# Nine of 256 softmax score units taken from ScalarE and computed on VectorE

## The chip, the cores and the metric

The kernel runs on one core of a Trainium2 chip. Its time is the device time of one execution in microseconds; most executions of one kernel agree within a few tenths of a per cent, but some, whatever the kernel, are some 3% longer. Medians below are over all executions of a kernel. A **ratio** is the mean time of one kernel's fast runs over the mean of the other kernel's fast runs of the same rounds, with a 95% interval, so it is not quite the ratio of the medians quoted beside it. "Span" is the time from the first to the last instruction of the one profiled execution; it is some 2 us below the time.

## The reference

Softmax attention over 64 heads of 512 x 64, in fp32:

```python
scale = 1.0 / np.sqrt(q.shape[-1])
scores = np.einsum('bhqd,bhkd->bhqk', q, k) * scale
scores = scores - scores.max(axis=-1, keepdims=True)
attn = np.exp(scores)
attn = attn / attn.sum(axis=-1, keepdims=True)
return np.einsum('bhqk,bhkd->bhqd', attn, v)        # 8 x 8 x 512 x 64
```

## The kernel before

Two heads make a pair; there are 32 pairs. A **unit** is one block of 128 keys against the 512 queries of one head: a 128x512 block of transposed scores, eight units to a pair, 256 in all. Three units make a group. TensorE writes the group's scores (`st`, two such buffers in PSUM, the memory that its results land in), ScalarE turns them into fp16 exponentials (`pt`) with one activation of 128x1536 into SBUF, the other on-chip memory, and TensorE later multiplies them with the values (`o`). VectorE copies transposed queries and keys out of PSUM (`tqk<-tps`) and normalises the outputs (`rcp`, `osb`); GpSimd casts the inputs to fp16.

```python
G = 3
def aux(shape, dt, name):                 # transposes AND outputs: two buffers, taken in turn
    return pspool.tile(shape, dt, tag="ps_x", bufs=2, name=name)
def scores(j):
    st[j] = pspool.tile([P, G, S], FP32, tag="ps_st", bufs=2, name=f"st_{j}")
    ...                                   # one matmul per unit into st[j][:, x, :]
def softmax(j):
    pt[j] = ppool.tile([P, G, S], FP16, tag="pt", name=f"pt_{j}")
    nc.scalar.activation(out=pt[j][:, 0:n], in_=st[j][:, 0:n], func=EXP, scale=scale)
def attend(g, h):
    o = aux([P, NI, W], FP32, f"o_{g}_{h}")
    weigh(g, h, o, range(NI))             # 16 matmuls pt x v; column 64 of v is 1: the sum
    normalise(g, h, o)                    # VectorE: reciprocal, then a multiply
...
for j, n in enumerate(sizes[:-1]):        # the program order of every engine
    softmax(j)
    scores(j + 1)
    ...                                   # work gets transposes and outputs as they fall due
    credit = min(credit + 0.42 * n, 2.0)
    while work and (credit >= 1.0 or j > len(sizes) - 6):
        f, *a = work.popleft(); f(*a); credit -= 1.0
```

The softmax here doesn't subtract the row's maximum and nothing guards it: scores larger than these inputs give would overflow.

## Time and profile before

| | before |
|---|---|
| time, median (lowest to highest) | 127.5 us (126.45 to 129.82), 3 runs |
| span of the profiled run | 125.1 us |
| ScalarE busy; idle before its exponentials | 117.5 us, 94%; 1.0 us |
| TensorE, VectorE, GpSimd busy | 107.2, 60.7, 58.9 us |

The prediction below shows the lines on which its reading rests. Two rows more, the busy tenths in 40 slices of the span, tell the room that the change wants to use. In this part of the page each digit is the busy share of one fortieth of the span, 9 meaning 90% or more:

```profile
DVE  0344536553653745445454554645546563553450
ACT  4499999999999999999999999999999999999970
```

ScalarE has no slice under 90% between the opening and the end, and VectorE stands at about half everywhere.

In an undisturbed stretch of this kernel activations start 1.33 us apart. From the starts in a trace I work out the **lateness**: the time between one full activation's start and the next, less 1.333 us, summed over all full groups but the first. It is 0.62 us for the kernel before. Three groups fewer save 4.03 us (the prediction's figure), so a changed kernel breaks even at a lateness of 0.62 + 4.03 = 4.65 us.

### The profile page before, as it was taken

The page shows a single profiled execution, that of the slowest core. Times are in us where ns is not written, and L with a number is a line of the kernel's source. Part 1 is how long each engine was busy: PE and PEld are TensorE (multiplying, and loading weights), DVE is VectorE, ACT ScalarE, POOL GpSimd, SP SyncE. Part 2 cuts the span into 40 slices and gives each one's busy share as a digit, 9 for nine tenths or more (in the row PEclk, how much of TensorE's full clock was granted, in tenths as well). Part 3 has the DMA queues.
Part 4 walks back from the last instruction along what each step waited for, and adds up shares of the span by engine and source line. Part 5 has one row for each costly group of instructions (what it writes and reads, how often), then busy time and mean ns, then how long its engine had stood idle before and what let it go on. Part 6 is the DMA issues. An engine that isn't in the chain of part 4 may idle for free.

```text
span 125.1 us, 3986 instructions
## 1 busy us (share of the span) xinstructions
PE 107.2 (86%) x1572; PEld 63.9 (51%) x1572; DVE 60.7 (49%) x173; ACT 117.5 (94%) x93; POOL 58.9 (47%) x101
## 2 busy tenths in 40 slices
PE   6999979889997987999798798979979898997780
PEld 6636536455464454565455265545536455554450
DVE  0344536553653745445454554645546563553450
ACT  4499999999999999999999999999999999999970
POOL 2188878576565173376347523644753753000000
PEclk9999999999999999999999999999999999999999
DMA  3999999999997699999789878989999974222222
GB/s 111 290 354 350 349 350 370 365 372 375 359 355 220 177 298 332 368 341 330 219 252 364 284 246 212 368 278 289 375 302 282 350 262 147 89 84 86 89 78 89
DMA packets 34882, 33.81 MB, mean 270 GB/s; under 512 B 2096, under 2 KB 34864, under 8 KB 34864
## 3 DMA queue, kind: packets, MB, share of 16 engines
q1 hardware_dynamic: 34576, 33.30, 82.0%
q8 instruction: 12, 0.20, 0.7%
q10 hardware_dynamic: 288, 0.26, 0.6%
q14 instruction: 6, 0.05, 0.1%
HBM read 25.17 MB, written 8.39 MB: 268 GB/s over the span
## 4 chain that ended last, share of the span: by engine, by line
ACT 74%; issue 16%; PE 4%; DMA 2%; DVE 1%
ACT pt L166 74%; DMA raw<-in_k_dram 2%; PE open L139 1%; PE st L161 1%; PE o_last L174 1%; PE o L174 0%; PE st L239 0%; DVE osb L188 0%; DVE x L135 0%; DVE rcp L187 0%
## 5 line engine op out<-in xcount | busy, mean ns | idle before, releaser
L166 ACT ACTIVATE pt<-st 128x1536 f16<-128x1536 f32 (+2 forms) x88 | 115.1, 1597 | 1.0 <-PE st L161 1.0
L161 PE MATMUL st<-tqk 64*128 64x512 f16 x248 | 49.6, 380 | 13.1 <-ACT pt L166 11.5
L174 PEld LDWEIGHTS <-pt 128*128 128x128 f16 x1024 | 33.8, 98 | 18.0 <-issue 16.2
L174 PE MATMUL o<-vp,pt 128*128 128x65 f16 x1008 | 38.4, 194 | 0.0
L91 POOL CAST qk<-q 128x512 f16<-128x512 f32 x31 | 19.1, 616 | 27.4 <-DMA q<-in_q_dram 19.6
L187 DVE RECIPROCAL rcp<-o 128x4 f32<-128x4 f32 x63 | 11.3, 180 | 38.8 <-PE o L174 38.8
L120 DVE COPY tqk<-tps 128x1024 f16<-128x1024 f16 (+1 forms) x32 | 21.5, 675 | 15.4 <-PE tps L119 15.4
L188 DVE TENSOR_TENSOR osb<-o,rcp 128x256 f32<-128x256 f32 x63 | 26.7, 425 | 2.2
L100 POOL CAST vp<-v 128x512 f16<-128x512 f32 x32 | 19.8, 619 | 10.6 <-DMA v<-in_v_dram 6.4
L161 PEld LDWEIGHTS <-tqk 64*128 64x128 f16 x248 | 11.6, 93 | 23.4 <-issue 14.8
L91 POOL CAST qk<-k 128x512 f16<-128x512 f32 x31 | 19.1, 616 | 5.6 <-DMA k<-in_k_dram 4.7
L119 PEld LDWEIGHTS <-qk 128*128 128x128 f16 x248 | 13.9, 98 | 13.1 <-issue 9.3
L119 PE MATMUL tps<-ident,qk 128*128 128x128 f16 x248 | 19.2, 220 | 0.0
L239 PE MATMUL warm<-blank 128*128 128x128 f16 x24 | 2.7, 310 | 1.0 <-DVE small L226 1.0
L239 PEld LDWEIGHTS <-blank 128*128 128x128 f16 x28 | 2.8, 142 | 1.2 <-DVE small L226 1.0
L227 ACT ACT_TABLE_LOAD x1 | 1.3, 1283 | 1.7 <-PEq L314 1.7
L161 PE MATMUL st<-t,r 64*128 64x512 f16 x6 | 2.0, 381 | 0.0
L139 PE MATMUL open<-ident,x 128*64 128x128 f16 x16 | 1.7, 268 | 0.2 <-DVE x L135 0.2
L135 DVE CAST x<-raw 128x192 f16<-128x192 f32 (+1 forms) x2 | 0.6, 284 | 2.5 <-DMA raw<-in_k_dram 2.5
L135 POOL CAST x<-raw 128x192 f16<-128x192 f32 x1 | 0.3, 344 | 3.0 <-DMA raw<-in_k_dram 3.0
L139 PEld LDWEIGHTS <-x 128*64 128x64 f16 x16 | 1.3, 138 | 0.9 <-DVE x L135 0.4
L144 DVE COPY t<-open 64x384 f16<-64x384 f16 (+1 forms) x2 | 0.8, 416 | 1.7 <-PE open L139 1.7
(20 smaller groups left out, 6.5 us busy)
## 6 DMA issues: line engine op xcount, KB each, us to landing
v<-in_v_dram SPq DMA_DIRECT2D x32, 256.0 KB, 5.6
q<-in_q_dram SPq DMA_DIRECT2D x31, 256.0 KB, 5.2
k<-in_k_dram SPq DMA_DIRECT2D x31, 256.0 KB, 5.6
out_dram<-osb SPq DMA_DIRECT2D x31, 256.0 KB, 4.8
raw<-in_k_dram ACTq DMA_DIRECT2D x2, 128.0 KB, 2.9
raw<-in_q_dram SPq DMA_DIRECT2D x2, 128.0 KB, 2.8
out_dram<-osb SPq DMA_DIRECT2D x2, 128.0 KB, 1.7
```

Source lines behind the costliest of these rows:

```text
L91: nc.gpsimd.tensor_copy(out=qk[:, n].rearrange("p i (h d) -> p i h d", d=D), in_=raw[g, "qk"[n]].rearrange("p h (i d) -> p i h d", d=D),)
L100: nc.gpsimd.tensor_copy(out=vps[g % NV][:, :, :, 0:D], in_=raw[g, "v"].rearrange("p h (i d) -> p h i d", d=D),)
L119: nc.tensor.transpose(ps[:, n - lo, i, :], halves[g][:, n, i, :], ident16)
L120: nc.vector.tensor_copy(out=turned[g][:, lo:hi], in_=ps)
L139: nc.tensor.transpose(ps[:, i - lo, :], raw["x", h][:, i, :], ident16)
L161: nc.tensor.matmul(st[j][:, x, :], key, tq, start=True, stop=True)
L166: nc.scalar.activation(out=pt[j][:, 0:n], in_=st[j][:, 0:n], func=EXP, scale=scale)
L174: nc.tensor.matmul(o[:, i, :], pt[j][:, x, i * P : (i + 1) * P], vps[g % NV][:, h, c, :], start=(c == 0 and i == blocks[0]), stop=(c == NI ...
L187: nc.vector.reciprocal(out=rcp[:, lo:hi], in_=o[:, lo:hi, D:W])
L188: nc.vector.tensor_tensor(out=o_sb[g][:, h, lo:hi], in0=o[:, lo:hi, 0:D], in1=rcp[:, lo:hi].broadcast_to([P, hi - lo, D]), op=AluOp.mult,)
L227: nc.scalar.activation(out=small, in_=small, func=EXP, scale=scale)
L239: nc.tensor.matmul(tile[:, G - 1, 0:P], blank, blank, start=True, stop=True)
```

## The change

Unit 0 of the first head of pairs 4, 7, ..., 28 leaves its group. Its scores go to one `aux` buffer and its exponential is made by five VectorE operations and one GpSimd operation: n is the exponent in half octaves (int8), e the bits of that power of two, f the fraction, and a, f2 and pa a cubic in f times the power. The work is begun two pairs ahead of the output that takes it, one step per group. It also puts a due transpose at the head of the queue of work and lets that queue run faster (0.5 for 0.42).

```diff
+    aside = [(g, 0, 0) for g in range(4, last, 3)]
+    units = [u for u in units if u not in aside]
...
+    def exp_aside(g):
...
+        s = aux([P, S], FP32, f"sa_{g}")
+        nc.tensor.matmul(s, tk[:, c * P : (c + 1) * P], tq, start=True, stop=True)
+        rate = 2.0 * scale * LOG2E
+        nc.vector.tensor_scalar(out=n, in0=s, scalar1=rate, scalar2=SHIFT, ...)        # n
+        nc.gpsimd.tensor_scalar(out=e, in0=n, scalar1=float(1 << 22), ...)             # e
+        step(f, s, rate, n, AluOp.mult, AluOp.subtract)                                # f
+        yield
+        step(a, f, EXP_P, f)                                                           # a
+        yield
+        step(f, f, EXP_R, e.bitcast(FP32))                                             # f2
+        yield
+        step(out16, a, EXP_Q, f)                                                       # pa
...
-                        work.append((transpose, g + 2))
+                        work.appendleft((transpose, g + 2))
+                    if r == 4 and any(a[0] == g + 2 for a in aside):
+                        work.append((begin_aside, g + 2))
...
-            credit = min(credit + 0.42 * n, 2.0)
+            while steps and next(steps[0], 1) == 1:      # one step, ahead of this group's work
+                steps.popleft()
+            credit = min(credit + 0.5 * n, 2.0)
```

More of the change, by code (lines that the diff above doesn't have):

```diff
@@ L11 @@
 FP16 = mybir.dt.float16
+I32 = mybir.dt.int32
+I8 = mybir.dt.int8
 EXP = mybir.ActivationFunctionType.Exp
 AluOp = mybir.AluOpType
+EXP_P, EXP_Q, EXP_R = 2.28771887, 28.39494972, 3.73321451
+SHIFT = -0.8899647686
+LEAD_BITS = 1008370304
+LOG2E = 1.4426950408889634
 @with_exitstack
@@ L47 @@
             units += [(g, c, h) for c in range(NI) for h in range(2)]
+    aside = [(g, 0, 0) for g in range(4, last, 3)]
+    units = [u for u in units if u not in aside]
     n_units = len(units)
+    first_of = {g: next(n for n, u in enumerate(units) if u[0] == g) for g in range(n_pairs)}
     G = 3
@@ L161, in scores, with tmp, step, begin_aside @@
             nc.tensor.matmul(st[j][:, x, :], key, tq, start=True, stop=True)
+    apart = {}
+    def exp_aside(g):
+        _, c, h = unit = next(u for u in aside if u[0] == g)
+        tq, tk = tqk[g, h]
+        def tmp(nm, dt=FP32):
+            return ppool.tile([P, S], dt, tag=nm, bufs=3, name=f"{nm}_{g}")
+        n, e, f, a = tmp("n", I8), tmp("e", I32), tmp("f"), tmp("a")
+        out16 = tmp("pa", FP16)
+        s = aux([P, S], FP32, f"sa_{g}")
+        nc.tensor.matmul(s, tk[:, c * P : (c + 1) * P], tq, start=True, stop=True)
+        rate = 2.0 * scale * LOG2E
+        nc.vector.tensor_scalar(
+            out=n, in0=s, scalar1=rate, scalar2=SHIFT, op0=AluOp.mult, op1=AluOp.add
+        )
+        nc.gpsimd.tensor_scalar(
+            out=e,
+            in0=n,
+            scalar1=float(1 << 22),
+            scalar2=float(LEAD_BITS),
+            op0=AluOp.mult,
+            op1=AluOp.add,
+        )
+        def step(o, x, k, y, op0=AluOp.add, op1=AluOp.mult):
+            nc.vector.scalar_tensor_tensor(out=o, in0=x, scalar=k, in1=y, op0=op0, op1=op1)
+        step(f, s, rate, n, AluOp.mult, AluOp.subtract)
[5 more added lines that the diff above has]
+        step(out16, a, EXP_Q, f)
+        apart[unit] = out16
+        yield
+    steps = deque()
+    def begin_aside(g):
+        steps.append(exp_aside(g))
+        next(steps[-1])
     def softmax(j):
@@ L171, in weigh @@
         for c in chunks:
-            j, x = where[g, c, h]
+            p = apart.get((g, c, h))
+            if p is None:
+                j, x = where[g, c, h]
+                p = pt[j][:, x]
             for i in blocks:
@@ L175, in weigh @@
                     o[:, i, :],
-                    pt[j][:, x, i * P : (i + 1) * P],
+                    p[:, i * P : (i + 1) * P],
                     vps[g % NV][:, h, c, :],
@@ L280 @@
                     g, c, h = units[u]
-                    r = u % UPP
+                    r = u - first_of[g]
                     if r == 0:
```

## The prediction

> **What bounds the kernel now.** I read the page's busy shares first, then the chain that ended last, the groups of instructions, and last the timeline of one steady stretch.
>
> ```profile
> PE 107.2 (86%) x1572; PEld 63.9 (51%) x1572; DVE 60.7 (49%) x173; ACT 117.5 (94%) x93; POOL 58.9 (47%) x101
> ...
> ACT 74%; issue 16%; PE 4%; DMA 2%; DVE 1%
> ...
> L166 ACT ACTIVATE pt<-st 128x1536 f16<-128x1536 f32 (+2 forms) x88 | 115.1, 1597 | 1.0 <-PE st L161 1.0
> L161 PE MATMUL st<-tqk 64*128 64x512 f16 x248 | 49.6, 380 | 13.1 <-ACT pt L166 11.5
> L187 DVE RECIPROCAL rcp<-o 128x4 f32<-128x4 f32 x63 | 11.3, 180 | 38.8 <-PE o L174 38.8
> L120 DVE COPY tqk<-tps 128x1024 f16<-128x1024 f16 (+1 forms) x32 | 21.5, 675 | 15.4 <-PE tps L119 15.4
> L188 DVE TENSOR_TENSOR osb<-o,rcp 128x256 f32<-128x256 f32 x63 | 26.7, 425 | 2.2
> ```
>
> ScalarE's exponentials are the bound: 94% busy, idle 1.0 us before 88 instructions, and they are the chain. Its 16% "issue" is the overlap of one activation with the next, not idling: the chain shows 1.0 us of an activation, then 0.3 of issue. Full groups of three units start at 65.67 us and, 39 groups later, at 118.07, so a group takes 52.4/39 = 1.344 us. VectorE is half idle, mostly for outputs of the matmuls. That is the room the change wants.
>
> But TensorE has less room than 86% suggests. This is its timeline, then VectorE's (start, length, instruction):
>
> ```profile
> 57.17 1.16 PE L174 MATMUL o<-vp,pt 128*128 128x65 f16 x32
> 58.27 0.60 PE L161 MATMUL st<-tqk 64*128 64x512 f16 x3
> 58.80 0.62 PE L119 MATMUL tps<-ident,qk 128*128 128x128 f16 x8
> 59.35 0.60 PE L161 MATMUL st<-tqk 64*128 64x512 f16 x3
> 60.68 0.59 PE L161 MATMUL st<-tqk 64*128 64x512 f16 x3 [0.73 <-ACT pt L166]
> ```
> ```profile
> 57.88 0.18 DVE L187 RECIPROCAL rcp<-o 128x4 f32<-128x4 f32 x1 [0.70 <-PE o L174]
> 58.09 0.42 DVE L188 TENSOR_TENSOR osb<-o,rcp 128x256 f32<-128x256 f32 x1
> 58.44 0.17 DVE L187 RECIPROCAL rcp<-o 128x4 f32<-128x4 f32 x1
> 58.64 0.42 DVE L188 TENSOR_TENSOR osb<-o,rcp 128x256 f32<-128x256 f32 x1
> 59.46 0.69 DVE L120 COPY tqk<-tps 128x1024 f16<-128x1024 f16 x1 [0.39 <-PE tps L119]
> ```
>
> The chain has activations starting at 54.93, 56.26, 57.59 and 58.96. Scores (st) have two buffers, so a group's scores start 0.385 us after the start of the activation that follows the buffer's reader (60.68 against 60.30), need 0.60 plus 0.09 to hand over, and must be ready 1.33 after that start. With 32 output matmuls between (57.17 to 58.27) the scores end at 58.87 and the activation starts at 58.96, 1.37 rather than 1.33 after the one before. So in those groups TensorE is already exactly on time: a delay there is lost to ScalarE one for one. Elsewhere slack is 0.2 to 0.7 us.
>
> **What the Trainium skill says.** "ScalarE: Activation LUTs", section "What ACT_TABLE_LOAD costs": 186 ns plus 0.833 ns an element, about 93 of it overlapping, so 1373 ns for 1536 elements; the trace has 1344, near enough, and nearly all per element, so fewer units pay in proportion. "VectorE: DVE Perf Modes", section "The TRN2 errata": fp32 tensor_tensor takes (N+151)/0.96 ns. For N=256 that is 424; the trace has 425. For N=512 I take 691 as an estimate from the same formula for all five added VectorE operations. "SBUF — State Buffer", section "Who interferes with whom": a VectorE operation with two SBUF inputs and a GpSimd operation that reads SBUF exclude one another for a whole instruction. The kernel before has no such large VectorE operation (its inputs come from PSUM), so its trace can't show this.
>
> **The change, part by part.** Removed: nine units leave ScalarE, 247 remain, 80 full groups for 83. Saved: 3 x 1.344 = 4.03 us, 3.2% of the span. Alone this gives 127.5 - 4.0 = 123.5.
>
> Added per aside: one score matmul (about 0.2 us), five VectorE operations of 0.69, 3.45 us, and one GpSimd operation which I take at a cast's 0.62. VectorE grows by 31 to about 92 us, 75%; but three pairs hold one aside, whose own load (6 normalisations of 0.6 and 3 copies of 0.69, 5.7 us) plus 3.45 is 9.1 of 23/3 x 1.33 = 10.2 us, 90%. GpSimd grows by 5.6 us and has time; it runs some pairs ahead of TensorE, so a wait for n costs it nothing that matters. Transfers run five pairs ahead and stay hidden.
>
> Moved: the aside's scores take one of only two PSUM buffers that transposes and outputs use in turn. So a transpose or output now waits for VectorE to finish with the aside two allocations earlier, and its in-order queue delays the copies and normalisations that free the others. The instruction order of the built kernel shows three patterns, each three times. I walk each with trace durations: a VectorE operation starts 0.04 after the matmul's end, 0.03 after one it depends on, 0.08 before the end of an independent one; TensorE follows VectorE by about 0.1. "Late" is against 1.33 a group.
>
> Pattern one (pairs 10, 19, 28): transpose, then the aside's scores at once, then a group's scores. Let the earlier group's scores start at 0; the next (1.33) is followed by the transpose at 1.85, copied 2.51 to 3.20. The aside's scores need that copy, so they start at 3.33 and hold the following group to 3.55, ready 4.24, due 3.605: **late 0.63**. Then n 3.75 to 4.44, f to 5.16, a to 5.88, normalisation of the first output to 6.43. The second output waits for that output's buffer: 6.53 to 7.08, then scores, ready 7.77, due 6.90: **late 0.87**.
>
> Pattern two (pairs 4, 13, 22): a group lies between transpose and aside, so the copy is nearly done. Aside at 1.98, n and f to 3.81, the second output waits until 3.91, group ready at 5.13, due 4.94: **late 0.20**. The next transpose waits for the normalisation behind a, but its group is ready at 6.42, due 6.46.
>
> Pattern three (pairs 7, 16, 25): it follows 32 output matmuls, so the transpose is late and the aside waits until 3.62. Groups ready 5.08 for 4.97, 6.77 for 6.41, and, since f2 stands before the next copy, 9.72 for 9.43: **late 0.11, 0.36 and 0.29**.
>
> Sum of one of each: 1.50 + 0.20 + 0.76 = 2.46 us. Nine pairs then take 23 x 1.33 + 2.46 + 0.1 (outputs as before) = 33.15 us, against 24 x 1.344 = 32.26. Times three: 2.7 us more, which gives 130.2. Port conflicts with the casts that GpSimd has queued behind e can only add; I give them 0.3.
>
> **The rivals.** First, all hidden: 123.5 us. For it: VectorE idles half of the time, each chain has over 5 us before its output, and a transpose now goes ahead of other work. Against it: that lead protects the finished exponential alone, not the PSUM buffers and the in-order queue in between, and ScalarE has only two score buffers. Second, a break-even near 127: my first lateness in pattern one is sure by the order, but the others depend on VectorE starting each operation at once and on 0.69 us; were these some 15% shorter, most of patterns two and three would vanish, leaving 3 x 1.4 against 4.0 saved. Someone chose nine units and these places, which speaks for a version that was at least no loss. Third, port conflicts in full: GpSimd has waited for n with two pairs' casts of 0.62 behind it, just where a, f2 and the last step run. A wait of up to 0.62 before a or f2 passes into the buffers; at 0.3 for each aside it adds 2.7 us, 133. Fourth, a bound by VectorE: 90% locally is below one, so it would show as waits, not as a full engine.
>
> **Range and chances.** I take 130.5 us. The range 126.0 to 134.0 reaches from most lateness absent to conflicts in full. Two per cent either way is 124.95 and 130.05. Faster needs under a quarter of the summed lateness (1.5 of 7.4 us), and pattern one's first wait alone takes 1.9: 0.08. Within 2% needs up to 2.55 us net loss, just under my sum: 0.42. Slower: 0.50.
>
> **What would show each step.** ScalarE should have 80 full activations and a busy time about 4 us lower, and its idle time before them, by score matmuls, should rise from 1.0 to some 7 us, in stretches of 0.2 to 0.9 near each aside, longest at pairs 10, 19 and 28. TensorE should wait for VectorE at the aside's scores, after a transpose's copy, and at outputs. VectorE's added operations should read near 0.69 us; if a, f2 and the last step read longer, or casts longer than 0.62, the port rule is at work. VectorE should be near 92 us. The prediction is wrong if ScalarE's idle stays under 3 us (buffers came free sooner than I walked), if the added operations are much shorter or longer, or if TensorE waits for GpSimd's casts or for transfers, which I left out.

## The result and the profile after

The changed kernel took 131.35 us (130.85 to 132.16, 4 runs), the kernel before on the same chip 127.17 (126.45 to 129.82, 4 runs). The ratio is 1.036 [1.029, 1.042]: slower by 3.6%.

From the page of the changed kernel: the busy shares, the two rows of tenths, the chain that ended last by engine, and five groups of instructions (busy us, mean ns, then idle before and what ended it).

```profile
PE 108.8 (84%) x1572; PEld 64.0 (49%) x1572; DVE 94.3 (73%) x218; ACT 115.7 (89%) x90; POOL 73.4 (57%) x110
...
DVE  0345579869967986996897599689779958974451
ACT  4499999999899699999997988999999899699970
...
DVE 41%; PE 32%; ACT 12%; issue 10%; DMA 2%; ACTq 0%
...
L226 ACT ACTIVATE pt<-st 128x1536 f16<-128x1536 f32 (+2 forms) x85 | 113.3, 1422 | 7.4 <-PE st L175 6.4
...
L205 DVE SCALAR_TENSOR_TENSOR f<-f,e 128x512 f32<-128x512 f32 x9 | 9.9, 1105 | 0.0
L205 DVE SCALAR_TENSOR_TENSOR pa<-a,f 128x512 f16<-128x512 f32 x9 | 9.5, 1057 | 0.0
L192 DVE TENSOR_SCALAR n<-sa 128x512 int8<-128x512 f32 x9 | 6.2, 692 | 4.3 <-PE sa L190 4.3
...
L205 DVE SCALAR_TENSOR_TENSOR a<-f 128x512 f32<-128x512 f32 x9 | 6.3, 706 | 0.2
```

The chain is no longer ScalarE's (74% before, 12% now) but runs through VectorE and TensorE. ScalarE waits 7.4 us for scores where it waited 1.0. VectorE's row now has nines, several in a row with eights: 73% is an average of full and half-empty slices. And f2 and pa take 1.1 us each where n, of the same 512 columns, takes 0.69.

Next, TensorE's waits in the changed kernel (what waited, for what: us in total, times, longest).

```profile
PE sa L190 <- DVE tqk L134: 3.9, 9, 0.8
PE tps L133 <- DVE rcp L250: 3.1, 9, 0.4
PE o L237 <- DVE f L205: 2.2, 6, 0.4
PE o L237 <- DVE tqk L134: 2.1, 6, 0.5
PE o L237 <- DVE osb L251: 2.0, 3, 0.7
```

In the kernel before, the same view had 0.3 us of waits for VectorE outside the opening (the scores for `tqk`) and 11.5 us of waits for ScalarE, which are the harmless ones. Here all but the first line are waits for an `aux` buffer.

Three timelines of the aside of pair 10, first TensorE, then VectorE, then GpSimd (start, length, instruction, idle before it):

```profile
40.03 0.39 PE L190 MATMUL sa<-tqk 64*128 64x512 f16 x1 [0.79 <-DVE tqk L134]
...
41.93 0.61 PE L133 MATMUL tps<-ident,qk 128*128 128x128 f16 x8 [0.15 <-DVE f L205]
43.21 0.67 PE L237 MATMUL o<-vp,pt 128*128 128x65 f16 x16 [0.68 <-DVE osb L251]
43.81 0.82 PE L175 MATMUL st<-tqk 64*128 64x512 f16 x6
```
```profile
40.45 0.69 DVE L192 TENSOR_SCALAR n<-sa 128x512 int8<-128x512 f32 x1 [0.48 <-PE sa L190]
41.18 0.69 DVE L205 SCALAR_TENSOR_TENSOR f<-sa,n 128x512 f32<-128x512 f32 x1
41.91 0.69 DVE L205 SCALAR_TENSOR_TENSOR a<-f 128x512 f32<-128x512 f32 x1
42.52 0.18 DVE L250 RECIPROCAL rcp<-o 128x4 f32<-128x4 f32 x1
42.73 0.42 DVE L251 TENSOR_TENSOR osb<-o,rcp 128x256 f32<-128x256 f32 x1
43.07 1.10 DVE L205 SCALAR_TENSOR_TENSOR f<-f,e 128x512 f32<-128x512 f32 x1
```
```profile
41.23 0.62 POOL L195 TENSOR_SCALAR e<-n 128x512 int32<-128x512 int8 x1 [4.49 <-PE o L237]
41.92 1.15 POOL L105 CAST qk<-q 128x512 f16<-128x512 f32 x1
43.02 0.61 POOL L105 CAST qk<-k 128x512 f16<-128x512 f32 x1
```

Read them together. The first output's matmuls are long done (they start at 40.57), but its normalisation stands behind n, f and a and ends at 43.15. Only then may the second output take that buffer, at 43.21; the scores that come after it on TensorE start at 43.81, and ScalarE's next activation starts at 44.51 after 0.98 us of idling. From n at 40.45 VectorE then works until 47.40 (46.98 + 0.42, its last normalisation) without a wait that the view lists; it is the same at pairs 19 and 28. GpSimd has stopped for n (4.49 us idle) and starts a row of casts at 41.92, some of which collide with a, f2 and pa: this q cast reads 1.15 us, f2 1.10.

By the activations' starts, the lateness rose from 0.62 to 9.19 us. More lateness 8.57, less 4.03 saved, is 4.5 us; the spans differ by 129.6 - 125.1 = 4.5. The account closes; what remains is which part of the aside makes the lateness. One candidate falls away by the trace: transposes did not wait for GpSimd's casts, although these come later than before. After the opening each cast of keys was done 3.3 us or more before the transposes that read it.

### The profile page after: what moved, and what is told of

Same layout as the page of the kernel before. It is cut to its first block, busy times and chain, and to the rows that moved or that the text cites. A ratio compares the mean times of both kernels' runs of the same rounds, so it can differ in the third digit from the quotient of the medians.

```text
span 129.6 us, 4031 instructions
## 1 busy us (share of the span) xinstructions
PE 108.8 (84%) x1572; PEld 64.0 (49%) x1572; DVE 94.3 (73%) x218; ACT 115.7 (89%) x90; POOL 73.4 (57%) x110
## 4 chain that ended last, share of the span: by engine, by line
DVE 41%; PE 32%; ACT 12%; issue 10%; DMA 2%; ACTq 0%
ACT pt L226 12%; PE st L175 10%; DVE f L205 10%; PE o L237 9%; DVE osb L251 9%; PE tps L133 8%; DVE tqk L134 7%; DVE pa L205 5%; DVE n L192 5%; DVE rcp L250 3%; PE sa L190 3%; DVE a L205 2%; DMA raw<-in_k_dram 2%; PE open L153 1%; PE o_last L237 1%
## 5 line engine op out<-in xcount | busy, mean ns | idle before, releaser
L175 PE MATMUL st<-tqk 64*128 64x512 f16 x239 | 47.6, 382 | 2.1 <-ACT pt L226 1.5
L105 POOL CAST qk<-q 128x512 f16<-128x512 f32 x31 | 25.0, 805 | 2.8 <-DMA q<-in_q_dram 1.8
L114 POOL CAST vp<-v 128x512 f16<-128x512 f32 x32 | 25.1, 786 | 0.6
L195 POOL TENSOR_SCALAR e<-n 128x512 int32<-128x512 int8 x9 | 5.6, 621 | 33.5 <-PE o L237 13.5
L205 DVE SCALAR_TENSOR_TENSOR f<-f,e 128x512 f32<-128x512 f32 x9 | 9.9, 1105 | 0.0
L205 DVE SCALAR_TENSOR_TENSOR pa<-a,f 128x512 f16<-128x512 f32 x9 | 9.5, 1057 | 0.0
L192 DVE TENSOR_SCALAR n<-sa 128x512 int8<-128x512 f32 x9 | 6.2, 692 | 4.3 <-PE sa L190 4.3
L190 PE MATMUL sa<-tqk 64*128 64x512 f16 x9 | 3.5, 387 | 3.9 <-DVE tqk L134 3.9
L205 DVE SCALAR_TENSOR_TENSOR a<-f 128x512 f32<-128x512 f32 x9 | 6.3, 706 | 0.2
L205 DVE SCALAR_TENSOR_TENSOR f<-sa,n 128x512 f32<-128x512 f32 x9 | 6.2, 692 | 0.3
## 6 DMA issues: line engine op xcount, KB each, us to landing
raw<-in_k_dram ACTq DMA_DIRECT2D x2, 128.0 KB, 2.9
raw<-in_q_dram SPq DMA_DIRECT2D x2, 128.0 KB, 2.7
out_dram<-osb SPq DMA_DIRECT2D x2, 128.0 KB, 1.7
```

The lines of the kernel that those rows point to most:

```text
L105: nc.gpsimd.tensor_copy(out=qk[:, n].rearrange("p i (h d) -> p i h d", d=D), in_=raw[g, "qk"[n]].rearrange("p h (i d) -> p i h d", d=D),)
L114: nc.gpsimd.tensor_copy(out=vps[g % NV][:, :, :, 0:D], in_=raw[g, "v"].rearrange("p h (i d) -> p h i d", d=D),)
L175: nc.tensor.matmul(st[j][:, x, :], key, tq, start=True, stop=True)
L190: nc.tensor.matmul(s, tk[:, c * P : (c + 1) * P], tq, start=True, stop=True)
L192: nc.vector.tensor_scalar(out=n, in0=s, scalar1=rate, scalar2=SHIFT, op0=AluOp.mult, op1=AluOp.add)
L205: nc.vector.scalar_tensor_tensor(out=o, in0=x, scalar=k, in1=y, op0=op0, op1=op1)
```

## The experiments

Theory: the lateness comes from VectorE's in-order queue together with the two `aux` buffers, as the walk in the prediction has it. Rivals: the port collisions with GpSimd (the two engines shutting one another out of SBUF, as the prediction has it); VectorE's load by itself; the aside's own matmul and PSUM buffer; the placing of the steps. Twelve runs, with the kernel before at 126.95 (first four), 127.18 (next three), 126.71 (next three) and 126.76 us (last two). Three are not in the table, as their profiled executions were slow or had a lowered clock: tail_gpsimd, one_read and steps_last.

| run | time, us | ratio | span | VectorE time of one aside | lateness |
|---|---|---|---|---|---|
| before | - | - | 125.1 | 0 | 0.62 |
| changed | 131.35 | 1.036 | 129.6 | 4.25 | 9.19 |
| all_short | 123.07 | 0.970 | 121.5 | 1.51 | 1.10 |
| tail_short | 126.22 | 0.995 | 124.1 | 2.59 | 3.97 |
| no_exponent | 129.92 | 1.024 | 128.0 | 3.91 | 8.01 |
| apart_turn | 130.42 | 1.025 | 128.4 | 4.47 | 8.17 |
| load_only | 128.15 | 1.011 | 126.8 | 4.03, no PSUM buffer | 2.07 |
| bits | 128.56 | 1.014 | 126.5 | 2.87 | 6.35 |
| bits_apart | 126.77 | 0.999 | 125.4 | 3.03 | 5.21 |
| one_step | 123.02 | 0.971 | 121.3 | 0.69 | 1.10 |
| bits_last | 125.52 | 0.991 | 124.2 | 3.01 | 4.06 |

The fifth column is the sum of the mean durations of the added VectorE operations. In every row the span differs from that of the kernel before by the added lateness less 4.03 (load_only: without that saving), to within 0.5 us. TensorE's waits for `aux` buffers go with the lateness: 9.9 us in the changed kernel, 7.2 in no_exponent, 6.2 in bits, 2.6 in tail_short, none in one_step. (In load_only 4.3 us of them cost less, 2.07 in all.)

### All steps short (all_short)

The order of the changed kernel, all six steps on 16 columns, the outputs fed from a fixed tile. Its output is wrong, which doesn't matter for the time.

```diff
-            return ppool.tile([P, S], dt, tag=nm, bufs=3, name=f"{nm}_{g}")
+            return ppool.tile([P, 16], dt, tag=nm, bufs=3, name=f"{nm}_{g}")
...
-        apart[unit] = out16
+        apart[unit] = fixed16
```

> Wrong result on purpose: the nine asides keep their matmul, their place and their buffers, but all six steps on VectorE and GpSimd work on 16 columns of 512, and the outputs take a fixed tile. My theory (the loss is TensorE waiting for VectorE, for the aside's own buffer and behind the aside's operations) leaves only the wait of the aside's scores for the transpose's copy, some 0.2 to 0.6 us in three or six of nine places: 124 to 126.5 us, faster than before. The rival, that the extra matmul out of its group and the lost order on TensorE cost it whatever VectorE does, expects 129 or more.

Measured: 123.07 us (122.81 to 123.28), ratio 0.970 [0.967, 0.973], better than the 124 to 126.5 expected. The aside's matmul, its buffer, its place in every queue and its number of instructions cost only 1.10 - 0.62 = 0.5 us of lateness. The saving of 4.0 us is real, and the loss is in the length of the steps.

### Only n and f long (tail_short)

n and f whole, the other four on 16 columns. Its output is wrong, which doesn't matter for the time.

```diff
-        step(a, f, EXP_P, f)
+        step(a[:, 0:16], f[:, 0:16], EXP_P, f[:, 0:16])
         (e, f2 and pa likewise; the outputs take the fixed tile)
```

> Wrong result on purpose: n and f, which read PSUM, stay whole; e, a, f2 and the last step work on 16 columns. By the same walk as in the prediction: pattern one 0.63 + 0.29, pattern two 0.20, pattern three 0.11 + 0.36, 1.6 us for three asides, 4.8 for nine, against 4.0 saved: about 128 us. If only the hold of the PSUM buffer by n and f counts, it stays at 130 to 131; if only the tail counts (its length and the port conflicts), it falls to 125 or below.

Measured: 126.22 us (125.93 to 126.47), ratio 0.995 [0.992, 0.999]; lateness 3.97. That is 1.8 us below the 128 of the walk. Lengthening n and f adds 2.9 us, and giving a, f2, pa and e their length adds the other 5.2.

### No GpSimd step (no_exponent)

The exponent's step left out, so GpSimd neither waits for n nor piles up casts; f2 takes a fixed tile for e. Its output is wrong, which doesn't matter for the time.

```diff
-        nc.gpsimd.tensor_scalar(out=e, in0=n, ...)
...
-        step(f, f, EXP_R, e.bitcast(FP32))
+        step(f, f, EXP_R, fixed)
```

> Wrong result on purpose: the GpSimd step is gone and f2 multiplies with a fixed tile, so GpSimd never stops for n and has no queue of casts behind it; all five VectorE operations stay whole. If the port conflicts (f2 at 1.10 and the last step at 1.05 us for 0.69) are the main loss, these fall to 0.69 and the time to 127 or below. My theory takes them for a smaller part: 2.5 us lateness for three asides as walked, 7.4 for nine, 130 us, with f2 and the last step somewhere between 0.69 and 1.1.

Measured: 129.92 us (129.76 to 133.87), ratio 1.024 [1.021, 1.027], as expected; lateness 8.01. Two rows of its groups:

```profile
L197 DVE SCALAR_TENSOR_TENSOR pa<-a,f 128x512 f16<-128x512 f32 x9 | 8.0, 887 | 0.0
L197 DVE SCALAR_TENSOR_TENSOR f<-f,fixed 128x512 f32<-128x512 f32 x9 | 7.5, 837 | 0.0
```

The two fall from 1057 and 1105 ns, not to 692, and a rises from 706 to 805; my reading is that ordinary casts still collide with them. The stop and the casts behind it cost 9.19 - 8.01 = 1.2 us. That is a part, and not the main one; what the collisions that are left cost, no run shows.

### The tail on GpSimd (tail_gpsimd)

A right result: f2 and pa as two GpSimd operations each, to take them off VectorE.

```diff
-        step(f, f, EXP_R, e.bitcast(FP32))
+        nc.gpsimd.tensor_scalar(out=f, in0=f, scalar1=EXP_R, scalar2=None, op0=AluOp.add)
+        nc.gpsimd.tensor_tensor(out=f, in0=f, in1=e.bitcast(FP32), op=AluOp.mult)
         (pa likewise)
```

> Right result: f2 and the last step go to GpSimd as two operations each[...], VectorE keeps n, f and a, 2.1 us for each aside. Walk: pattern one 1.50, two 0.20, three 0.47, 2.2 us for three asides, 6.5 for nine against 4.0 saved: 129.5 us. If GpSimd gets too late with its casts (5.6 + 0.6 + 3.4 = 9.6 us for three pairs of 10.3) then TensorE's transposes wait for it and the time is 131 or above.

Measured: 156.41 us (151.82 to 160.5); all its runs had a lowered clock (0.89 in the profiled one), so no ratio is given. A miss by 20%, and the profile says why:

```profile
L211 POOL TENSOR_SCALAR f<-f 128x512 f32<-128x512 f32 x9 | 13.5, 1497 | 0.0
...
L212 POOL TENSOR_TENSOR f<-f,e 128x512 f32<-128x512 f32 x9 | 11.4, 1269 | 0.7
```

I had taken 0.62 us from GpSimd's casts; with fp32 in these operations take 1.27 to 1.50, while the casts in the same run still take 0.62 to 0.72. GpSimd is busy for 114 us and TensorE waits 17.8 us for pa. GpSimd has no room for this.

### The steps after the group's work (steps_last)

The next step of a begun aside stands behind the normalisations and copies of its group instead of before.

```diff
-            while steps and next(steps[0], 1) == 1:
-                steps.popleft()
+            begun = len(steps)
...                                  (after the loop over work)
+            if begun and next(steps[0], 1) == 1:
+                steps.popleft()
```

> Right result, same instructions and same load of VectorE as the changed kernel; only a, f2 and the last step stand at the end of their group's work, not at its head, so in pattern one a comes after the first output's normalisation and in pattern three f2 after the transpose's copy. My theory (an in-order VectorE in front of PSUM buffers) takes about 0.7 us off each pattern one and 0.7 to 1.0 off each pattern three, 4.2 to 5 us in all: 126 to 127.5 us. If VectorE's load as such is the loss, wherever it stands, it stays at 130 to 131.

Measured: 130.54 us, ratio 1.026 [1.022, 1.031]. Three runs lie between 130.01 and 130.73; the fourth, which is the profiled one, took 229.26 with 512-column score matmuls of 723 ns instead of 382, so its trace is not used. Less than 1% better than the changed kernel, where 126 to 127.5 us was expected: a miss.

### No aside in a transpose's group (apart_turn)

As steps_last, and an aside is put off by a group where a transpose has just been made, so its scores do not wait for that copy.

```diff
+                if work[0][0] is begin_aside and turned_now:
+                    break
```

> Right result; as the run with the steps last, and an aside no longer begins in the group that has a transpose, so its scores do not stand on TensorE right behind the copy that they need (pattern one becomes like pattern three). Theory: 0.2 to 0.6 us less for each of the three places: 0.6 to 1.8 us below the run with the steps last. If that wait is hidden anyway, no difference.

Measured: 130.42 us (129.69 to 132.97), ratio 1.025 [1.019, 1.031]; lateness 8.17, now in many pieces, most of 0.2 to 0.6 us. It is 0.1 us from steps_last, where 0.6 to 1.8 was expected. a, f2 and pa read 1.00, 1.07 and 1.02 us: later steps meet more casts (my reading). VectorE works from 28.48 to 36.5 us with one gap of 0.19, and in front of outputs TensorE's weight loads wait 4.6 us for pa, its matmuls 1.7. Moving the steps moved the lateness; neither of the two places tried had 4.5 us of VectorE to spare.

### One read of PSUM (one_read)

As apart_turn, but VectorE only copies the scaled scores to SBUF and GpSimd makes n from the copy, so the `aux` buffer is free after 0.7 us.

```diff
-        nc.vector.tensor_scalar(out=n, in0=s, ...)
+        nc.vector.tensor_scalar(out=xs, in0=s, scalar1=rate, scalar2=None, op0=AluOp.mult)
+        nc.gpsimd.tensor_scalar(out=n, in0=xs, scalar1=SHIFT, scalar2=None, op0=AluOp.add)
```

> As the run before it in this list, but VectorE reads the aside's scores from PSUM once (a scaled copy to SBUF, 0.69 us) and n is made from that copy on GpSimd, so the buffer is held for 0.69 instead of 1.4 us; VectorE still has five operations. The run with a short tail had 4.0 us of lateness in all, most of it by this hold; halved it should give 1 to 2 us: 123.5 to 125.5 us, faster than before. The result may fail the comparison if GpSimd rounds to int8 in another way; the time counts all the same. If the hold is not what counts, the time is that of the run before it.

Measured: 143.99 us (141.27 to 149.19), clock 0.89 in the profiled run. A miss of the same kind as tail_gpsimd: n on GpSimd takes 1498 ns, e comes some 1.5 us later, and TensorE waits 11.8 us for pa. It tells nothing about the buffer.

### The load alone (load_only)

The kernel before, with 45 idle VectorE operations on SBUF at about the places of the steps (the first two stand at the head of a group's work, where n and f follow the aside's matmul in the queue): no unit moved, no matmul, no PSUM buffer, no GpSimd step.

```diff
+    def load_steps(n):
+        for _ in range(n):
+            nc.vector.tensor_tensor(out=idle[1], in0=idle[0], in1=idle[0], op=AluOp.mult)
...
+                    if r == 4 and g in range(2, last - 2, 3):
+                        owed += [2, 1, 1, 1]
+            if owed:
+                load_steps(owed.pop(0))
```

> Right result. The kernel before, its 256 units on ScalarE and its order on TensorE unchanged; nine times five VectorE operations of 128x512 on a private SBUF tile stand where the aside's stand (two, one, one, one a group). No PSUM buffer, no matmul, no GpSimd step. It measures what VectorE's load costs by itself. If the load in VectorE's queue is the loss, as the runs with the steps moved suggest (no gain from moving them), lateness is 4 to 6 us as in the changed kernel less its hold of PSUM, and nothing is saved: 130.5 to 133 us. If the loss needs the aside's own buffer, it stays within 1 us of before.

Measured: 128.15 us (127.73 to 128.56), ratio 1.011 [1.008, 1.014]: below the 130.5 to 133 of a loss by load, and a little over the 1 us of the other case.

```profile
L156 DVE TENSOR_TENSOR idle<-idle 128x512 f32<-128x512 f32 x45 | 36.3, 807 | 0.6
```

36.3 us of VectorE work, about what the asides add (9 x 4.25 = 38, or 9 x 3.91 = 35 without the GpSimd step), costs 1.45 us of lateness, against 7.4 added in no_exponent. Neither the load alone (1.45) nor the aside's matmul and buffer with short steps (0.5, all_short) makes the lateness, nor do the two added up (1.9). Together they cost far more. My reading: with one more user of two buffers each must come back sooner, and the same queue brings each back later.

### Another exponential (bits)

Right result (the exponential within 0.24% rms, worked out on the host): the scores become the bits of a power of two as int32, the mantissa is masked out, and a quadratic of it corrects the straight line. Four VectorE operations, one read of PSUM, none on GpSimd.

```diff
+        nc.vector.tensor_scalar(out=b, in0=s, scalar1=scale * LOG2E * (1 << 23), scalar2=BIAS_BITS, ...)
+        yield
+        nc.vector.tensor_scalar(out=m, in0=b, scalar1=0x7FFFFF, scalar2=0x3F800000,
+                                op0=AluOp.bitwise_and, op1=AluOp.bitwise_or)
+        nc.vector.scalar_tensor_tensor(out=a, in0=m32, scalar=QUAD_P, in1=m32, ...)
+        yield
+        nc.vector.scalar_tensor_tensor(out=out16, in0=a, scalar=QUAD_Q, in1=b.bitcast(FP32), ...)
```

> Right result hoped for (0.24% rms error in nine units). Another exponential in the changed kernel's place: VectorE writes the float's bits as an integer (one read of PSUM, 0.69 us), masks the mantissa, and takes a quadratic in it, four operations, about 2.5 us, and nothing on GpSimd, so no casts queue up and the buffer is held for 0.69 us instead of 1.4. The run with a short tail had VectorE operations of about the same sum and 4.0 us of lateness with the long hold. So 2 to 3.5 us of lateness against 4.0 saved: 124 to 126.3 us. If only the number of asides' matmuls or the order counted, it would be near 130.

Measured: 128.56 us (128.31 to 132.25), ratio 1.014 [1.011, 1.016]. Better than the changed kernel by 2%, worse than before, and a miss (124 to 126.3 expected). Note against tail_short: bits reads PSUM once, 2.87 us an aside, and is late by 6.35; tail_short reads it twice, 2.59 us, and is late by 3.97. This suggests that the second read, which holds the buffer for f, is not the main cost, and that m and a, which stand together in front of the group's work here, cost as well; the two runs differ in more than one thing.

### Another exponential, asides put off (bits_apart)

bits with the asides put off as in apart_turn (the same two lines), the steps still ahead of the group's work.

> As the run with the bits, and no aside begins in a transpose's group. Removes TensorE's wait for the transpose's copy in three of nine places: 0.2 to 0.6 us each; 0.5 to 1.5 us below that run, 123 to 125.5 us. No difference if that wait was hidden.

Measured: 126.77 us (126.21 to 130.43), ratio 0.999 [0.994, 1.003]: level with the kernel before, and short of what I expected. Here, with a queue that is less full, the placing takes 1.1 us off the lateness.

### One step only (one_step)

A coarser result that still passes the comparison with the reference: the scores times 1024 log2(e)/8 plus 15300 are written as int16, and those bits are read as fp16, a straight line between powers of two. Order and places as in the changed kernel.

```diff
+        nc.vector.tensor_scalar(out=b, in0=s, scalar1=scale * LOG2E * 1024.0,
+                                scalar2=15360.0 - 60.0, ...)          # b is int16
+        out16 = b.bitcast(FP16)
```

> The changed kernel with its order, but each aside is one VectorE operation and nothing on GpSimd: the scores times 1024 log2(e)/8 plus 15300 are written as int16 and those bits are read as fp16, a straight line between powers of two (worked out on the host: relative error of the nine heads' outputs 0.9%, of the whole output 0.33%). My theory, that the lateness comes from what follows the first operation (the buffer held for f, and a, f2, pa and the GpSimd step in the full queue): near the run with all steps on 16 columns (123.07), plus n at full length, so 123.0 to 124.8 us, ratio 0.97 to 0.98, ScalarE late by 1.2 to 2.5 us in all, and the one operation near 0.69 us. The rival, that the first operation and the aside's PSUM buffer of two already cost most of it: 125.5 us or more.

Measured: 123.02 us (122.71 to 127.16, 6 runs), ratio 0.971 [0.969, 0.974], faster by 2.9% and as expected. From its page the busy shares and two groups, then TensorE's waits:

```profile
PE 107.3 (89%) x1572; PEld 63.6 (52%) x1572; DVE 66.7 (55%) x182; ACT 113.8 (94%) x90; POOL 58.7 (48%) x101
...
L208 ACT ACTIVATE pt<-st 128x1536 f16<-128x1536 f32 (+2 forms) x85 | 111.4, 1467 | 0.9 <-PE st L177 0.9
...
L192 DVE TENSOR_SCALAR b<-sa 128x512 int16<-128x512 f32 x9 | 6.2, 692 | 4.3 <-PE sa L191 4.3
```
```profile
PE st L177 <- ACT pt L208: 4.0, 17, 0.7
PE sa L191 <- DVE tqk L136: 3.9, 9, 0.8
```

Set this against the waits of the changed kernel. The wait of the aside's scores for the transpose's copy is the same, 3.9 us in 9 times, and here it costs next to nothing: lateness is 1.10, as with all steps short. The waits for `aux` buffers (`o` and `tps` for VectorE) are gone, and ScalarE is 94% busy again. So the first full-length operation on the aside's scores is free, and the ones after it are not. The loss went together with the buffer waits; as VectorE's load and GpSimd's stop went too, this run alone does not part them.

### The exact version with the steps last (bits_last)

bits_apart, and the steps moved behind the group's work as in steps_last (the same lines).

> The precise exponential of four VectorE operations, no aside begun in a transpose's group, and now the steps at the end of a group's work, so that both normalisations go before m, a and pa. If TensorE's waits for a normalisation behind those steps were what was left of the lateness (5.2 us in the run without this): 124.5 to 126 us, ratio 0.98 to 0.99. If, as with the steps moved in the earlier runs, VectorE is simply full in that stretch and pa then comes late for its output: 126.5 to 128 us, no better than the kernel before.

Measured: 125.52 us (125.09 to 129.04, 6 runs), ratio 0.991 [0.988, 0.994]; lateness 4.06, just under break-even. The two longest of its four operations:

```profile
L202 DVE SCALAR_TENSOR_TENSOR pa<-a,b 128x512 f16<-128x512 f32 x9 | 7.9, 883 | 0.0
L200 DVE SCALAR_TENSOR_TENSOR a<-m 128x512 f32<-128x512 f32 x9 | 7.7, 850 | 0.3
```

The time is in the expected range. This is a version with an accurate exponential that beats both kernels, by 0.9% (clear of the noise, if under 2%) and some 4%. Long pieces of lateness remain, of 0.66 and 0.61 us (at 45.5 and 47.4 us), 0.74 (66.9) and 0.80 (98.6). At the first of them TensorE's second output waits 0.64 us for a normalisation that stands behind m and a, so the exact version still has something to gain from its order.

## Why the prediction was right

The prediction gave 130.5 us, 126 to 134, and slower as the likeliest, at 0.50; the time was 131.35. The loss was under-sized by about a third: 3.0 us forecast, against 4.5 by the spans. Point by point:

- **The saving, 4.03 us: right.** all_short and one_step, which have it with almost no lateness, have spans 3.6 and 3.8 us shorter. ScalarE's busy time fell by 3.7 us in both, but only by 1.8 in the changed kernel, not by the 4 that I named as a sign: an activation that begins after a gap has no predecessor to overlap with. (My reading; no run tests it. An estimate from the trace fits: 21 activations start over 0.1 us late, one after a gap lasts 1.45 us where the pitch is 1.33, and 21 x 0.12 = 2.5 us is about the 2.2 that are missing.)
- **ScalarE's idle to some 7 us: right**, 7.4.
- **Pattern one (pair 10 and its like), 0.63 + 0.87: the sum near, the parts not.** Measured 0.20 + 1.09. The first part, which I called sure by the order, was over-sized: the wait of the aside's scores for the copy is there in full (0.79 us) yet costs 0.2, in one_step too. The second went link for link as walked: n, f, a, normalisation, output, scores. From the aside's matmul the second activation comes after 4.48 us, walked 4.44. The first part shows in the trace as three terms. The scores before the transpose start 0.22 us after their activation (38.09 against 37.87), not 0.385; the aside follows them after 1.94, not 2.00; and it holds the next group not at all, where I gave it 0.22. Score matmuls of the two heads, 64 rows each, start in twos, under 0.01 us apart, and the next two 0.22 later. A group of three leaves one alone, and here the aside's joins the group's first: four start as two pairs, and the activation comes 0.71 us after the first of them, against 0.70 for a group of three (58.27 to 58.96 in the kernel before). That these two run side by side is my reading of it.
- **Pattern two, 0.20: measured 0.26 to 0.41.**
- **Pattern three, 0.76: measured 1.33** (0.17, 0.22, 0.69, 0.25). This is the largest miss of a term. The walk took 0.69 for every operation; f2 and pa took 1.1. The third part, walked as 0.29 because f2 stands before the next copy, became 0.69: f2 is longer by 0.41, and the output waits for that copy (at pair 7 for 0.51 us, from 33.16 to 33.67). By the prediction's own signs ("much shorter or longer") this was a warning, for two of five operations.
- **Port collisions, 0.3 us: four times too small.** no_exponent puts those from GpSimd's stop and its queued casts at 1.2. The sign that I had named, f2, pa and some casts longer than 0.69 and 0.62, is plain. Whether all collisions together come near the third rival's 2.7 us is not shown, as no_exponent keeps those with ordinary casts.
- **VectorE near 92 us: 94.3.** (The 75% beside it was loose: 92 of some 128 us are 72%; measured 73%.) Its operations take the 0.69 that I assumed where nothing blocks them: n and f 692 ns, a 706.
- **The fourth rival, a bound by VectorE, was put aside too quickly.** "90% locally is below one, so it would show as waits" is true of the mean, but for 7 us after each aside of pattern one the engine has no gap. This fits that putting the steps elsewhere (steps_last, apart_turn) gained under 1%, while making them fewer did gain: at 1.5 us an aside and less the lateness is 0.5 above the kernel before, at 2.6 to 3.0 it is 3.4 to 5.7, at 3.9 and more 7.4 to 8.6 (load_only, without a buffer, apart).

Sum: the terms make 7.4 + 0.3, the trace 9.2 less the 0.6 that was there before. The mechanism held; it was under-sized in pattern three and in the collisions and over-sized in the first wait of pattern one. That these errors partly cancel, so that the time came within 1 us, is luck. The 1373 and 424 ns of the prediction are estimates by the formulas that it names; the 1344 beside the first is the pitch, of activations that last 1642 ns and overlap by 0.30 us.

One thing stays open. How load and buffers multiply was shown by taking each alone, not by a run that has the load and a buffer but no dependence of one on the other; and no run changes the number of `aux` buffers, which would test it directly.

## What to carry to other kernels

Room on an engine is not its idle share: an in-order engine that frees shared buffers gives away only what it can spare between two buffers that others are waiting for. Here the first 0.7 to 1.5 us of VectorE time an aside cost next to nothing, and the next 2.7 cost twice what the whole change earned, so the way to a gain was a shorter substitute (one operation; or four without the second engine, which gained only with better places as well: bits alone lost 1.4%), not a better place for the long one. Test the room before writing the work: the same instructions on 16 columns show the price of the order, dummy operations that of the load, and neither alone shows that of both.

## What the Trainium skill lacked or had wrong

- "GPSIMD Engine Reference", section "3.1 Elementwise — side-by-side cycle accounting": its best case, for one input as I read it, is 768 ns for 512 elements. A tensor_scalar of 128x512 from fp32 took 1490 to 1498 ns here (nine instructions at each of three places in two kernels), twice as long, while int8 to int32 took 617 to 621 (1009 in one_read) and undisturbed casts of fp32 to fp16 616, both below that best case. The section lacks a figure by operation and type. Its 2.6 cycles an element for two inputs (1109 ns as an estimate from that section, at 1.2 GHz) is nearer: 1264 to 1269 measured.
- "SBUF — State Buffer", section "Who interferes with whom": right that the operations with two SBUF inputs collide with GpSimd's casts. It speaks of slower measurements, but lacks what a trace shows: the blocked instruction isn't shown as idle but as longer, f2 1.10 us for 0.69 and a q cast 1.15 for 0.62, so collisions hide in busy time. And it lacks the mean price: 0.4 us for f2 and pa behind a queue of casts, 0.15 to 0.2 with casts spread out (no_exponent).
- "TensorE: Matmul & The Clock Gate", section "Seeing it yourself": it warns that the recorded clock events are unreliable and that the gate has been seen stuck for over 50 us. One of the 4 executions of steps_last goes further: score matmuls of 723 ns instead of 382, about half their rate, over the whole 227 us span, while the recorded clock is 1.0 in it. Why that execution was slow is not known; a reader should judge such a run by the duration of a matmul, not by the clock.
